# A hybrid encoder block with a gathered expert layer: how its place tiles are made, how many parked groups run per query tile, and how its weights and rows are buffered

## The chip, the cores and the metric

The kernel runs on one core of one Trainium2 chip. The metric is device microseconds (us) of one execution. TensorE is PE in the profile (PEld is its weight load), VectorE is DVE, ScalarE is ACT, GpSimd is POOL, SyncE is SP.

## The reference

One encoder layer on 1024 tokens of width 1024: adaLN, two token mixers (grouped attention and a bidirectional state-space scan) merged by gates, then a PEER expert layer, then a last norm. The part that matters here is PEER:

```python
q = (xt @ w_query).reshape(T, 8, 2, 128)
s1, s2 = scores of both halves of q against 128 keys each      # per head
v1, i1 = top_k(s1, 16); v2, i2 = top_k(s2, 16)
sc, pos = top_k(all sums v1 + v2, 16)                          # 16 of 16384 experts
idx = (i1 * 128 + i2)[pos];  g = softmax(sc)
a = gelu(einsum('thkd,td->thk', u_tab[idx], xt))
out = einsum('thk,thkd->td', g * a, v_tab[idx])
```

## The kernel before, in words

All products of weights and activations are made in three products of halves (`mm3`, L192): a float32 operand is split into a high part (ACT, a cast) and a low part (source less high part, on POOL or DVE), and PE adds high x high, high x low and low x high. `weights` (L178) loads one 128 x 1024 weight tile in two half loads through `wr` (three buffers) and splits it into whole tiles `wh` and `wl` (two buffers each).

PEER treats the tokens in two ways. The first TB = 384 tokens (three blocks of 128) are *fetched*: for each of 128 slots, POOL gathers one row of u for each token (128 x 1024, 512 KB) into a row buffer `br`, DVE makes the dot product with the token's activations (L1189), and after all slots rows of v are gathered four at a time and added by PE (`add`, L1220). The generator `fetched` (L1156) writes this order: a gather is written when the list `ahead` of unread rows holds no more than NROW - 1 = 8, with NROW = 9 buffers.

The other 640 tokens are *dense*: all 16384 experts, as 128 chunks of 128, are computed for all of them. `hidden_parts(c)` (L1303) makes gelu(u h) of a chunk in four parts, a quarter of its 48 matmuls of 320 columns each; the two halves of the tokens (j) one after the other, each with its own PSUM tile `hb`. Its weights are loaded two chunks ahead: `load` (L1293) at a chunk's end, and the low halves (`lows`) in the middle of the next. 88 chunks (PARKED, L72, spread evenly over the 128) are made early as filler and stored to `a_d` (L1325); the others are made when they are used.

The stages around the change: (1) query tiles, L1421: for each of 16 tiles m, two products of the query, the scores of the tile before, and four parts of a parked chunk. (2) the top 16 per score on DVE (`top`, L991) and the routing of blocks (`route`, L1034: DVE with products `ro` on POOL, L1085). (3) placing, L1482: the routed experts of four tokens become a one-hot pair of tiles `quad` (L1329): DVE compares a row of 0..127 (`iota`, which lies in PSUM) with both coordinates of all four tokens in one instruction over 1024 columns; then the second half is weighted by the gate (`weighted`, L1335), on POOL for two quads of four (one instruction over 512 columns), on ACT for the others (four of 128). PE multiplies the pair (`place`, L1342), ACT copies the result to `stg`, and 64 tokens at a time go to `G_d`. GB = 6 `quad` buffers. (4) the last stage, L1580 on: groups of EG = 3 chunks, each a live or parked chunk times its places, times v, added to `acc`; the fetching goes on beside it.

PE, DVE and POOL run in the order in which the program is written in stages 1 to 3 (`manual`, L1404), DVE and POOL in stage 4. That order comes from a planner with three clocks, at_pe, at_dve and at_dma: each written piece adds its assumed time (a part 1.73, a routing step ROUTE 2.5, a top TOP 1.8, a quad QUAD 1.7, a gather DGET 1.6). `hide` (L1386) writes parts of parked chunks while PE's clock is behind DVE's, until all but HOLD = 8 parts are written; `follow` (L1406) writes tops and routing steps while DVE's is behind PE's; `feed` (L1356) writes gathers while the transfers' clock is behind both, once the first block is routed, and adds 1.25 to DVE's clock for a u row and 0.46 to PE's for a v row.

Of the kernel before, what the change touches and what calls it, by code (L numbers as in the profile page):

```python
# [20 lines left out]
D = 1024  # L21
# [8 lines left out]
CUTS = [(0, TQ)] + [(TQ + j * W2, W2) for j in range(NJ)]  # L30
# [3 lines left out]
NPARK = 88  # L34
BSTEP = 3
FSTEP = 2
NROW = 9
# [4 lines left out]
QPOOL = 2  # L42
# [6 lines left out]
GB = 6  # L49
# [10 lines left out]
WH = 2  # L60
WL = 2
# [10 lines left out]
PARKED = [c for c in range(128) if (c + 1) * NPARK // 128 > c * NPARK // 128]  # L72
# [46 lines left out]
def block(ctx, tc, A, out, dbg=None):  # L119
# [58 lines left out]
    def weights(src, kd, eng=None, late=None):  # L178
        hi = wp.tile([128, 8, 128], FR, name="wh", bufs=WH)
        lo = wp.tile([128, 8, 128], FR, name="wl", bufs=WL)  # L180
        for k in range(0, kd, 4):
            raw = wp.tile([128, 4, 128], F32, name="wr", bufs=WR)
            nc.sync.dma_start(raw, src[:, k:k + 4])
            if late is None:
                split(raw, hi[:, k:k + 4], lo[:, k:k + 4], eng and eng[k // 4])
                continue
            ACT.copy(hi[:, k:k + 4], raw)  # L187
            late.append(lambda k=k, raw=raw: ((eng and eng[k // 4]) or POOL).tensor_tensor(  # L188
                lo[:, k:k + 4], raw, f32(hi[:, k:k + 4]), op=OP.subtract))
        return hi, lo  # L190
# [606 lines left out]
    bg = bp.tile([128, NB, 128], F32, name="bg")  # L797
    hx = pool("hx")
# [157 lines left out]
    kr = rt.tile([128, N_KR], F32, name="kr")  # L956
    nc.sync.dma_start(kr, A["kr"])
    for nm, x in zip("hl", (xh, xl)):
        for p, a in zip(x, others(nm, FR)):
            p[1] = a  # L960
    h2h, h2l = ([x[m][1] for m in range(8)] for x in (xh, xl))
    ip = pool("ip", "right")
    bw = pool("bw", "right")
    best = [bw.tile([128, 4, 2, 8, 16], F32, name="best", bufs=2) for _ in range(2)]
# [69 lines left out]
    def route(blk):  # L1034
# [66 lines left out]
        if blk < NB:  # L1101
            V.tensor_copy(bidx[:, blk], exf)
            V.tensor_copy(bx[:, blk], exf)
            V.tensor_copy(bg[:, blk], gf)
            ready.append(blk)
            yield
            return
# [19 lines left out]
    def final(p, src, t0, n, x1):  # L1127
        tl = slice(t0, t0 + n)
        nc.sync.dma_start(x1, x1_d[:, :, tl])
        yield "w"  # L1130
        yield "w"
        yield "w"
        for m in range(8):
            V.scalar_tensor_tensor(x1[:, m], src[:, m // 4, m % 4], mod[:, 40 + m:41 + m], x1[:, m], op0=OP.mult, op1=OP.add)
        yield "w"
        o = wide()
        acc = o[:, 0]
        for m in range(0, 8, 2):
            some = []
            for _ in range(2):  # L1140
                some.append(p.tile([128, n], F32, name="fsq", bufs=2))
# [12 lines left out]
        nc.sync.dma_start(out[:, :, tl], x1)  # L1154

    def fetched():  # L1156
# [5 lines left out]
        def rows(tab, idx):  # L1162
            r = rt.tile([128, D], F32, name="br", bufs=NROW)
# [8 lines left out]
        for b in range(NB):  # L1172
# [4 lines left out]
            yield from drain(NROW - 1)  # L1177
            st = rt.tile([128, D], F32, name="br", bufs=NROW)
            nc.sync.dma_start(st, h2t_d[b])
# [18 lines left out]
            def weights_of(b=b, a=a, aT=aT):  # L1198
                ACT.activation(a, a, AF.Gelu_apprx_tanh)
                yield "w"  # L1200
                V.tensor_tensor(a, a, bg[:, b], op=OP.mult)
# [4 lines left out]
                PE.transpose(o[:, :128], a, ident)  # L1206
                ACT.copy(aT, o[:, :128])

            ahead.append((1, begin))
            for s in range(128):  # L1210
                yield from drain(NROW - 1)
                r = rows("u", bidx[:, b, s:s + 1])
                ahead.append((1, lambda s=s, r=r, dot=dot: dot(s, r)))
                if s == 96:
                    flipped()
# [4 lines left out]
            def add(i, R, aT=aT, acc=acc):  # L1220
# [3 lines left out]
                if i % VG == 0:  # L1224
                    ACT.copy(z[:, :, 31:31 + 32 * VG:32], aT.rearrange("p (g i) -> p g i", g=4)[:, :, i:i + VG])
                at = 31 + 32 * (i % VG) - i
                for h in range(2):
                    for g in range(4):
                        PE.matmul(acc[0][32 * g:32 * g + 32, h], lhsT=z[:, g, at:at + 32], rhs=R[g][:, h * 512:(h + 1) * 512],  # L1229
                                  start=(i == 0), stop=(i == 31))  # L1230
# [3 lines left out]
            def finish(b=b, acc=acc):  # L1234
# [8 lines left out]
                x1 = rt.tile([128, 8, 128], F32, name="bacc")  # L1243
                yield from final(rt, o, b * 128, 128, x1)

            for i in range(32):
                R = []
                for g in range(4):
                    yield from drain(NROW - 1 - g)
                    R.append(rows("v", ixt[:, 32 * g + i:32 * g + i + 1]))  # L1250
# [26 lines left out]
    la.release()  # L1277
    dn = pool("dn")
# [3 lines left out]
    sources = [x for m in range(16) for x in (A["wq"][m], A["uT"][order[m]])] + [A["uT"][c] for c in order[16:]]  # L1282
# [10 lines left out]
    def load():  # L1293
        lows()
        src = next(sources, None)
        if src is not None:
            loaded.append(weights(src, 8, halves_by, late))

    load()
# [3 lines left out]
    def hidden_parts(c):  # L1303
        uh, ul = loaded.popleft()
        a = dn.tile([128, TA], F32, name="a", bufs=2)
        done = 0
        for j in range(NJ):
            o = psE.tile([128, 512], F32, name="hb", bufs=2)[:, :W2]
            js = slice(j * W2, (j + 1) * W2)
            for kd in range(8):  # L1310
                mm3(o, (uh[:, kd], ul[:, kd]), (h2h[kd][:, js], h2l[kd][:, js]), kd == 0, kd == 7)
                done += 1
                if done == 4 * NJ:
                    lows()
# [20 lines left out]
    def weighted(x, ig, t):  # L1335
        if t // 4 % 4 < QPOOL:
            POOL.tensor_tensor(x[:, 1], x[:, 1], ig[:, 2, t:t + 4].unsqueeze(2).to_broadcast([128, 4, 128]), op=OP.mult)
        else:
            for j in range(4):
                ACT.activation(x[:, 1, j], x[:, 1, j], AF.Identity, scale=ig[:, 2, t + j:t + j + 1])  # L1340
# [80 lines left out]
    for m in range(17):  # L1421
# [15 lines left out]
        if m < 16:  # L1437
            for _ in range(4):
# [42 lines left out]
    compared = []  # L1481
    for t in range(TB, S, 4):  # L1482
        blk = t // 128
        made.append((t - TB, quad(crossed[blk], t % 128)))
        if compared:
            weighted(*compared.pop())
        compared.append((made[-1][1], crossed[blk], t % 128))
# [7 lines left out]
    weighted(*compared.pop())  # L1495
# [133 lines left out]
    for m in range(8):  # L1629
        x1 = rt.tile([128, TA], F32, name="br", bufs=NROW)  # L1630
# [4 lines left out]
    def last(m, j, js, o):  # L1635
        x = acc[:, m, js]
        V.scalar_tensor_tensor(x, o, mod[:, 40 + m:41 + m], x, op0=OP.mult, op1=OP.add)
        sq = rt.tile([128, W2], F32, name="br", bufs=NROW)
# [14 lines left out]
    dn.release()  # L1653
    hx.release()
# [64 lines left out]
```

## Time and profile before

| what | value |
|---|---|
| runs shown, median (lowest, highest) | 4068.97 us (4056.01, 4076.5), three runs |
| the profiled execution, its time | 4056.31 us |
| its span | 4054.5 us |
| mean granted clock of PE | 0.953 |
| busy, share of the span | PE 90%, DVE 64%, POOL 45%, ACT 33% |
| 16 transfer engines | 211 GB/s over the span, 854 MB |

A busy time is the time in which an engine had at least one instruction running. A wait is the idle time of an engine in front of an instruction, put down to what ended last before it. In the tables of windows the count of instructions stands in brackets, and the granted clock is a share of full speed.

### The profile page before, as it was taken

The numbers are of one execution on the slowest core, as the hardware profiler recorded it, in microseconds if no ns is written. First come the engines' busy times: TensorE is split into PE (matmuls) and PEld (weight loads), VectorE is DVE, ScalarE is ACT, GpSimd is POOL, SyncE is SP. The second block draws the span as 40 slices with busy tenths as digits, with TensorE's granted clock in tenths as the row PEclk, the third lists the DMA queues.
The fourth block names the chain that finished last, engine by engine and source line by source line (L and its number), as shares of the span: only waits on it lengthen the run. The fifth ranks groups of instructions, "written<-read, shape, count | busy, mean of one in ns | idle before, by whom it ended". The sixth has DMA issues, their size and how long they took to land.

```text
span 4054.5 us, 61036 instructions
## 1 busy us (share of the span) xinstructions
PE 3660.2 (90%) x22927; PEld 3204.8 (79%) x22927; DVE 2578.8 (64%) x5316; ACT 1339.1 (33%) x2659; POOL 1812.5 (45%) x1529
## 2 busy tenths in 40 slices
PE   5799999998899899679888888999999899999998
PEld 4577777776688799678677788999788899978887
DVE  5698951347672678934785556489444698864456
ACT  4265542223323432122225655422222222222222
POOL 3211112565454567736776545444444343434420
PEclk8899999998899999789998999999999999999999
DMA  5111124323375349944776777888898798889962
GB/s 182 37 46 46 50 89 142 109 92 121 116 231 175 104 165 318 346 164 148 252 250 209 269 270 273 313 284 297 315 315 309 251 314 284 298 293 318 312 231 87
DMA packets 387784, 854.04 MB, mean 211 GB/s; under 512 B 32800, under 2 KB 146976, under 8 KB 384672
## 3 DMA queue, kind: packets, MB, share of 16 engines
q1 hardware_dynamic: 276896, 447.44, 32.5%
q0 software_dynamic: 110592, 402.70, 28.6%
q8 instruction: 180, 2.95, 0.3%
q14 instruction: 116, 0.95, 0.1%
HBM read 740.44 MB, written 109.58 MB: 210 GB/s over the span
## 4 chain that ended last, share of the span: by engine, by line
PE 33%; DVE 9%; DMA 8%; issue 2%; ACT 2%; POOL 2%; SPq 0%; ACTq 0%; POOLq 0%; DVEq 0%
PE pb L195 4%; PE pb L194 4%; PE pb L196 4%; PE hb L194 4%; DMA vr<-v 4%; PE hb L196 4%; PE gx L1229 4%; PE hb L195 4%; PE pb L1346 3%; DVE br L1189 3%; DMA G_d<-stg 2%; PE io L194 1%; PE io L195 1%; DVE Wl L1545 1%; PE io L196 1%
## 5 line engine op out<-in xcount | busy, mean ns | idle before, releaser
L196 PE MATMUL hb<-ah,wl 128*128 128x320 f32 x2048 | 649.3, 317 | 59.5 <-POOL wl L188 41.1
L194 PE MATMUL hb<-ah,wh 128*128 128x320 f32 x2048 | 661.1, 323 | 19.3 <-ACT a L1317 19.1
L195 PE MATMUL hb<-al,wh 128*128 128x320 f32 x2048 | 646.4, 316 | 0.0
L1164 POOL DMA_INDIRECT br<-u,bidx x384 | 366.5, 955 | 470.0 <-DVE br L1189 330.1
L1164 POOL DMA_INDIRECT br<-v,ixt x384 | 381.1, 992 | 425.9 <-PE gx L1229 303.4
L174 POOL TENSOR_TENSOR wl<-wr,wh 128x512 fp32r<-128x512 f32 x170 | 230.0, 1367 | 673.1 <-ACT wh L173 617.7
L194 PE MATMUL pb<-Wh,vh 128*128 128x320 f32 x1536 | 473.6, 315 | 16.3 <-ACT Wh L1542 11.8
L195 PE MATMUL pb<-Wl,vh 128*128 128x320 f32 x1536 | 479.0, 313 | 9.5 <-DVE Wl L1545 9.4
L196 PE MATMUL pb<-Wh,vl 128*128 128x320 f32 x1536 | 476.3, 311 | 0.0
L1189 DVE SCALAR_TENSOR_TENSOR br<-br,gx 128x1024 f32<-128x1024 f32 x384 | 454.9, 1215 | 30.3 <-DMA br<-u,bidx 27.7
L196 PEld LDWEIGHTS hb<-ah,wl 128*128 128x128 f32 x2048 | 396.8, 194 | 67.3 <-POOL wl L188 45.1
L194 PEld LDWEIGHTS hb<-ah,wh 128*128 128x128 f32 x2048 | 398.2, 194 | 48.9 <-issue 24.0
L188 POOL TENSOR_TENSOR wl<-wr,wh 128x512 fp32r<-128x512 f32 x269 | 343.2, 1296 | 201.2 <-ACT wh L187 198.7
L195 PEld LDWEIGHTS hb<-al,wh 128*128 128x128 f32 x2048 | 397.8, 194 | 0.0
L1575 DVE TENSOR_TENSOR acc<-acc,pb 128x320 f32<-128x320 f32 x492 | 229.8, 485 | 209.1 <-PE pb L196 207.8
L187 ACT CAST wh<-wr 128x512 fp32r<-128x512 f32 x288 | 177.1, 618 | 560.4 <-DMA wr<-uT 303.9
L173 ACT CAST vh<-vr 128x512 fp32r<-128x512 f32 x256 | 150.9, 618 | 614.1 <-PE pb L195 395.1
L194 PEld LDWEIGHTS pb<-Wh,vh 128*128 128x128 f32 x1536 | 288.1, 190 | 43.5 <-ACT Wh L1542 16.7
L195 PEld LDWEIGHTS pb<-Wl,vh 128*128 128x128 f32 x1536 | 290.7, 189 | 17.7 <-DVE Wl L1545 14.2
L1331 DVE TENSOR_TENSOR quad<-io,rig 128x1024 f32<-128x1024 f32 x160 | 190.4, 1221 | 166.6 <-PE pb L1346 105.1
L196 PEld LDWEIGHTS pb<-Wh,vl 128*128 128x128 f32 x1536 | 290.4, 189 | 0.2
L194 PE MATMUL w<-hh,wh 128*128 128x512 f32 x560 | 230.1, 411 | 8.2 <-ACT zg L548 4.3
(362 smaller groups left out, 8235.6 us busy)
## 6 DMA issues: line engine op xcount, KB each, us to landing
wr<-uT SPq DMA_DIRECT2D x256, 256.0 KB, 4.5
vr<-v SPq DMA_DIRECT2D x256, 256.0 KB, 5.7
G_d<-stg SPq DMA_DIRECT2D x20, 2048.0 KB, 12.2
gt<-G_d SPq DMA_DIRECT2D x42, 960.0 KB, 6.5
a_d<-a SPq DMA_DIRECT2D x88, 320.0 KB, 4.4
a<-a_d SPq DMA_DIRECT2D x88, 320.0 KB, 5.9
wr<-wi SPq DMA_DIRECT2D x82, 256.0 KB, 2.7
sq<-adaT SPq DMA_DIRECT2D x32, 512.0 KB, 4.3
```

What stands on the lines that cost most here:

```text
L173: ACT.copy(hi, src)
L174: (eng or POOL).tensor_tensor(lo, src, f32(hi), op=OP.subtract)
L187: ACT.copy(hi[:, k:k + 4], raw)
L188: late.append(lambda k=k, raw=raw: ((eng and eng[k // 4]) or POOL).tensor_tensor(lo[:, k:k + 4], raw, f32(hi[:, k:k + 4]), op=OP.subtract))
L194: PE.matmul(o, lhsT=wh, rhs=xh, start=first, stop=False)
L195: PE.matmul(o, lhsT=wh, rhs=xl, start=False, stop=False)
L196: PE.matmul(o, lhsT=wl, rhs=xh, start=False, stop=last)
L1164: POOL.indirect_dma_start(out=r, out_offset=None, in_=A[tab], in_offset=bass.IndirectOffsetOnAxis(ap=idx, axis=0))
L1189: V.scalar_tensor_tensor(v2(r), v2(r), 1.0, hrow[0], op0=OP.mult, op1=OP.mult, accum_out=a[:, s:s + 1])
L1229: PE.matmul(acc[0][32 * g:32 * g + 32, h], lhsT=z[:, g, at:at + 32], rhs=R[g][:, h * 512:(h + 1) * 512], start=(i == 0), stop=(i == 31))
L1331: V.tensor_tensor(x, iota.unsqueeze(1).unsqueeze(1).to_broadcast([128, 2, 4, 128]), ig[:, 0:2, t:t + 4].unsqueeze(3).to_broadcast([128, 2, ...
L1575: V.tensor_tensor(acc[:, m, js], acc[:, m, js], o, op=OP.add)
```

## The change

With TB = 384 the new constant TH is 0, so all code under `if TH`, and the branches for a half block in `fetched` and `final`, are never taken; CUTS keeps its values. What is left:

- `quad` makes the first half with one compare over 512 columns and the second with one compare-and-multiply of 128 columns per token, all on DVE; `weighted` is gone; GB is 5.
- PARKED is every chunk but the first of each group of three: 85 instead of 88. Eight parts are written per query tile, not four, and `sources` has two chunks after each query tile.
- `wh` and `wl` are half tiles with four buffers each. `hidden_parts` runs the first half of the weights for both j, then the second half for both; a half is reloaded when both j have used it.
- NROW is 10, and the list `ahead` may hold NROW - 1 - SLACK = 7. The row buffers lie in a pool `rg` of their own.

```diff
-NROW = 9
+NROW = 10
+SLACK = 2
-GB = 6
+GB = 5
-WH = 2
-WL = 2
+WH = 4
+WL = 4
-PARKED = [c for c in range(128) if (c + 1) * NPARK // 128 > c * NPARK // 128]
+PARKED = [c for c in range(128) if c % EG]
+NPARK = len(PARKED)
...
+    def weight_half(src, k, hi, lo, eng=None, late=None):
+        raw = wp.tile([128, 4, 128], F32, name="wr", bufs=WR)
+        nc.sync.dma_start(raw, src[:, k:k + 4])
+        h = wp.tile([128, 4, 128], FR, name="wh", bufs=WH)
+        w = wp.tile([128, 4, 128], FR, name="wl", bufs=WL)
...
+        ACT.copy(h, raw)
+        late.append(lambda: (eng or POOL).tensor_tensor(w, raw, f32(h), op=OP.subtract))
...
-                yield from drain(NROW - 1)
-                r = rows("u", bidx[:, b, s:s + 1])
+                yield from drain(NROW - 1 - SLACK)
+                r = rows("u", at_idx[:, s:s + 1])
...
-    sources = [x for m in range(16) for x in (A["wq"][m], A["uT"][order[m]])] + [A["uT"][c] for c in order[16:]]
+    sources = [x for m in range(16) for x in (A["wq"][m], A["uT"][order[2 * m]], A["uT"][order[2 * m + 1]])]
+    sources += [A["uT"][c] for c in order[32:]]
...
-        for j in range(NJ):
-            o = psE.tile([128, 512], F32, name="hb", bufs=2)[:, :W2]
+        turn[0] = NJ - 1 - turn[0]
+        first = [abs(turn[0] - j) for j in range(NJ)]
+        o = {}
+        parts = [(j, k) for k, js in ((0, first), (1, first[::-1])) for j in js]
+        for n, (j, k) in enumerate(parts):
+            if not k:
+                o[j] = psE.tile([128, 512], F32, name="hb", bufs=2)[:, :W2]
             js = slice(j * W2, (j + 1) * W2)
-            for kd in range(8):
-                mm3(o, (uh[:, kd], ul[:, kd]), (h2h[kd][:, js], h2l[kd][:, js]), kd == 0, kd == 7)
-                done += 1
-                if done == 4 * NJ:
-                    lows()
-                if done % (2 * NJ) == 0 and done < 8 * NJ:
-                    yield None
-            ACT.activation(a[:, js], o, AF.Gelu_apprx_tanh)
-        load()
-        yield a
+            for kd in range(4 * k, 4 * k + 4):
+                mm3(o[j], (uh[:, kd], ul[:, kd]), (h2h[kd][:, js], h2l[kd][:, js]), kd == 0, kd == 7)
+            if k:
+                ACT.activation(a[:, js], o[j], AF.Gelu_apprx_tanh)
+            if n in (0, 2):
+                lows()
+            if n in (1, 3):
+                load(n // 2)
+            yield a if n == 3 else None
...
-        V.tensor_tensor(x, iota.unsqueeze(1).unsqueeze(1).to_broadcast([128, 2, 4, 128]),
-                        ig[:, 0:2, t:t + 4].unsqueeze(3).to_broadcast([128, 2, 4, 128]), op=OP.is_equal)
+        V.tensor_tensor(x[:, 0], iota.unsqueeze(1).to_broadcast([128, 4, 128]),
+                        ig[:, 0, t:t + 4].unsqueeze(2).to_broadcast([128, 4, 128]), op=OP.is_equal)
+        for j in range(4):
+            V.tensor_scalar(x[:, 1, j], iota, ig[:, 1, t + j:t + j + 1], ig[:, 2, t + j:t + j + 1], op0=OP.is_equal, op1=OP.mult)
...
-            for _ in range(4):
+            for _ in range(8):
                 parked_part()
                 follow(0.0)
```

## Rows read from the trace of the kernel before

**Rows 1.** Windows by stage: busy time of each engine (instructions), PEclk, DMA share, GB/s.

```profile
1500.00:1600.00 100.00, 98.57 (x689) 98.30 (x688) 89.76 (x315) 29.16 (x66) 75.45 (x71) 1.00 0.90 314
1600.00:1650.00 50.00, 34.29 (x222) 34.02 (x221) 45.74 (x132) 9.65 (x21) 33.78 (x35) 0.83 0.89 332
1700.00:1750.00 50.00, 28.56 (x163) 28.03 (x162) 45.76 (x173) 6.30 (x12) 32.34 (x33) 0.73 0.88 343
1905.00:2146.00 241.00, 207.86 (x1341) 166.69 (x1341) 177.05 (x565) 58.50 (x113) 191.95 (x149) 0.94 0.74 243
2146.00:2570.00 424.00, 372.01 (x2753) 347.77 (x2754) 250.86 (x280) 246.92 (x754) 232.69 (x221) 0.92 0.72 260
2660.00:2850.00 190.00, 178.13 (x1182) 174.65 (x1181) 167.41 (x299) 45.32 (x79) 75.89 (x75) 0.99 0.87 292
2850.00:3200.00 350.00, 347.43 (x2395) 289.51 (x2394) 172.98 (x296) 75.85 (x139) 151.58 (x148) 1.00 0.89 309
```

**Rows 2.** Waits of PE, 1320 to 1905 us: total, times, longest.

```profile
PE pb L196 <- POOL wl L188: 32.9, 3, 15.7
PE hb L196 <- POOL wl L188: 22.9, 3, 14.0
```

**Rows 3.** Instructions of POOL in order of time, 1608 to 1638 us: start, length.

```profile
1608.23 0.95 POOL L1164 DMA_INDIRECT br<-u,bidx  x1
...
1633.08 0.94 POOL L1164 DMA_INDIRECT br<-u,bidx  x1 [0.31 <-DVE best L995]
1634.04 3.74 POOL L188 TENSOR_TENSOR wl<-wr,wh 128x512 fp32r<-128x512 f32 x3
```

**Rows 4.** Waits of DVE, 1700 to 1905 us.

```profile
DVE re L1078 <- POOL ro L1085: 107.6, 4, 102.6
```

**Rows 5.** Stores of parked chunks on SP's queue, in order of time: start, length.

```profile
1443.81 0.42 SPq L1325 DMA_DIRECT2D a_d<-a  x1
...
1466.59 0.33 SPq L1325 DMA_DIRECT2D a_d<-a  x1
...
1481.79 0.33 SPq L1325 DMA_DIRECT2D a_d<-a  x1
...
1758.31 0.40 SPq L1325 DMA_DIRECT2D a_d<-a  x1
...
1864.03 0.33 SPq L1325 DMA_DIRECT2D a_d<-a  x1
```

**Rows 6.** Waits of PE, 1905 to 2146 us.

```profile
PE hb L196 <- DVE wl L188: 17.2, 7, 5.5
PE hb L196 <- POOL wl L188: 9.6, 9, 1.9
```

**Rows 7.** Groups of instructions, whole span: busy us, mean ns, idle before and what ended it.

```profile
L1189 DVE SCALAR_TENSOR_TENSOR br<-br,gx 128x1024 f32<-128x1024 f32 x384 | 454.9, 1215 | 30.3 <-DMA br<-u,bidx 27.7 <-ACT gx L1184 2.2
...
L1331 DVE TENSOR_TENSOR quad<-io,rig 128x1024 f32<-128x1024 f32 x160 | 190.4, 1221 | 166.6 <-PE pb L1346 105.1 <-issue 26.2 <-ACT quad L1340 11.1
...
L1317 ACT ACTIVATE a<-hb 128x320 f32<-128x320 f32 x256 | 109.3, 434 | 184.0 <-PE hb L196 77.3 <-issue 54.8 <-DVE Wl L1545 39.9
...
L1340 ACT ACTIVATE quad<-quad,rig 128x128 f32<-128x128 f32 x320 | 103.5, 398 | 23.1 <-DVE quad L1331 22.7
...
L1189 DVE DVE_READ_ACCUMULATOR br<-br,gx 128x1 f32 x384 | 32.2, 84 | 0.0
```

**Rows 8.** Waits of PE, 2146 to 2570 us.

```profile
PE pb L1346 <- ACT stg L1349: 28.7, 8, 5.3
...
PE pb L1346 <- POOL quad L1337: 8.4, 1, 8.4
```

**Rows 9.** Line 207, VectorE reading PSUM: ns min/median/max, first and last start, shapes.

```profile
L207 DVE TENSOR_SCALAR rstd<-pb x8: 248/420/426, 26.6 to 1322.9; 128x256 f32<-128x256 f32 x6, 128x96 f32<-128x96 f32 x1, 128x160 f32<-128x160 f32 x1
L207 DVE TENSOR_SCALAR rstd<-gx x3: 181/184/185, 2410.3 to 3935.4; 128x32 f32<-128x32 f32 x3
```

**Rows 10.** Instructions of VectorE in order of time, from 2401 us.

```profile
2401.37 2.16 DVE L1134 SCALAR_TENSOR_TENSOR bacc<-gx,mod,bacc 128x128 f32<-128x128 f32 x8 [2.01 <-DMA bacc<-x_d]
```

More of the change, by code (lines that the diff above doesn't have):

```diff
@@ L41 @@
 TOP = 1.8
-QPOOL = 2
 RSTEPS = 18
@@ L797, in block @@
     bg = bp.tile([128, NB, 128], F32, name="bg")
+    if TH:
+        hidx = bp.tile([128, 64], I32, name="hidx")
+        hg = bp.tile([128, 64], F32, name="hg")
     hx = pool("hx")
@@ L960, in block @@
             p[1] = a
+            if TH:
+                (ACT.copy if nm == "h" else POOL.tensor_copy)(a[:, :TQ - TB], f32(p[0])[:, TB:])
     h2h, h2l = ([x[m][1] for m in range(8)] for x in (xh, xl))
@@ L963, in block @@
     bw = pool("bw", "right")
+    kr = bw.tile([128, N_KR], F32, name="kr")
+    nc.sync.dma_start(kr, A["kr"])
     best = [bw.tile([128, 4, 2, 8, 16], F32, name="best", bufs=2) for _ in range(2)]
@@ L1140, in final @@
             for _ in range(2):
-                some.append(p.tile([128, n], F32, name="fsq", bufs=2))
+                some.append(p.tile([128, 128], F32, name="fsq", bufs=2)[:, :n])
                 ACT.activation(some[-1], x1[:, m + len(some) - 1], AF.Square)
@@ L1176, in fetched @@
             aT = rt.tile([128, 128], F32, name="aT")
-            yield from drain(NROW - 1)
-            st = rt.tile([128, D], F32, name="br", bufs=NROW)
-            nc.sync.dma_start(st, h2t_d[b])
+            yield from drain(NROW - 1 - SLACK)
+            st = rg.tile([128, D], F32, name="br", bufs=NROW)
+            half = 128 * b + 128 > TB
+            if half:
+                for k in range(2):
+                    nc.sync.dma_start(st[64 * k:64 * k + 64], h2t_d[b, 0:64])
+            else:
+                nc.sync.dma_start(st, h2t_d[b])
+            at_idx, at_g = (hidx, hg) if half else (bidx[:, b], bg[:, b])
+            slots = 64 if half else 128
             hrow = []
@@ L1242, in finish @@
                     PE.transpose(o[:, m // 4, m % 4], s[:, m * 128:(m + 1) * 128], ident)
-                x1 = rt.tile([128, 8, 128], F32, name="bacc")
-                yield from final(rt, o, b * 128, 128, x1)
-            for i in range(32):
+                x1 = rt.tile([128, 1024], F32, name="bacc")[:, :8 * n].rearrange("p (m t) -> p m t", m=8)
+                yield from final(rt, o, b * 128, n, x1)
+            for i in range(steps):
                 R = []
                 for g in range(4):
-                    yield from drain(NROW - 1 - g)
-                    R.append(rows("v", ixt[:, 32 * g + i:32 * g + i + 1]))
+                    yield from drain(NROW - 1 - SLACK - g)
+                    R.append(rows("v", ixt[:, steps * g + i:steps * g + i + 1]))
                     yield "v"
@@ L1291, in lows, with load @@
             late.pop(0)()
-    def load():
-        lows()
-        src = next(sources, None)
-        if src is not None:
-            loaded.append(weights(src, 8, halves_by, late))
+    def load(half=None):
+        if half != 1:
+            src = next(sources, None)
+            if src is not None:
+                loaded.append((Halves(), Halves()))
+                coming.append(src)
+        for k in (0, 1) if half is None else (half,):
+            lows()
+            if coming:
+                weight_half(coming[0], 4 * k, *loaded[-1], halves_by and halves_by[k], late)
+                if k:
+                    coming.pop()
+    coming = []
     load()
@@ L1653, in block @@
     dn.release()
+    rg.release()
     hx.release()
```

93 lines of the change are left out of this document (49 added, 44 removed).

## The prediction

> **What bounds the kernel now.** I read the windows by stage first [rows 1]. From 1500 to 1600 us TensorE (PE) is 98.6% busy; then it falls to 34.3 of 50 us and 28.6 of 50 us at a granted clock of 0.83 and 0.73, and VectorE (DVE) is busy for over 90% of these two windows. In routing (1905 to 2146) and placing (2146 to 2570) no engine is full: placing has PE at 372.0, DVE at 250.9 and ScalarE (ACT) at 246.9 of 424 us. In the last stage PE is full again: idle 11.9 us of 190 where u rows are fetched and 2.6 us of 350 where v rows are. So what can be won lies between 1600 and 2570 us.
>
> The waits of PE say why it starves there: 32.9 us in three waits of a query tile and 22.9 us in three waits of a chunk for `wl`, the low half of a split weight, made by POOL [rows 2]. The POOL list shows what `wl` stands behind: a run of 21 u gathers from 1608.23 to 1633.08, one per 1.24 us, then three splits at once [rows 3]. DVE has the opposite hole a little later, 107.6 us in four waits for POOL's `ro` product [rows 4]: there the list of POOL holds the splits of some sixteen chunks that PE runs back to back, one per 7.05 us [rows 5]. The two holes are one fault of order: too little PE work was written into the query tiles, so the planner first writes gathers in a bunch and then chunks in a bunch.
>
> I walked the planner's sums through the code (part 1.73, ROUTE 2.5, TOP 1.8, DGET 1.6). Before, 53 u gathers are issued by the end of the 12th tile and 115 by the 16th, 15 a tile at the end; 64 parts are written in the tile loop and 65 more during the 15 scores left over. After, the gathers stand at 19, 56, 93 and 129 after 4, 8, 12 and 16 tiles, 9 a tile, and 128 of the 133 parts that are written by then stand inside the loop.
>
> **The change part by part.** The sum is made against the profiled execution, 4056.3 us (span 4054.5); the median of the runs, 4069.0, is 12.7 us above it.
>
> *Two chunks per query tile.* Before, the store of the first parked chunk starts at 1443.81 and that of the 32nd at 1864.03: 420.2 us [rows 5]. A tile with one chunk takes 15.20 us (1466.59 to 1481.79) and a chunk alone 7.05 (15 steps from 1758.31 to 1864.03), so a tile with two takes 22.25 us if PE stays full. The 32nd store is then 7.05 + 15 x 22.25 = 340.8 us behind the first: 79 us won. The other bound is transfers: a tile moves three weight tiles (1.57 MB), two stores (0.66) and 9.1 gathers of 0.52 MB (4.79), 7.02 MB; at the 292 GB/s of 2660 to 2850 [rows 1] that is 24.0 us a tile, and 53 us won; at the 314 and 343 GB/s of 1500 to 1750 it is 22.4 and 20.5, no more than PE's time. POOL has 9.1 x 1.24 + 6 x 1.25 = 18.8 us of work per tile plus its share of `ro`, so it has little slack either. I take 23.6 us, near the slow end: 361 us, **59 won**. DVE does the same list in it, without the 107.6 us hole. The four half loads and the store that each added chunk issues move past nothing but other weight loads on SP's queue; they are in the 7.02 MB.
>
> *Half weight tiles, and the order of the four parts.* A chunk's first half is now reloaded after its second part, and its split is due five parts before its use, not two. In the query stage this is part of the 59. In routing the waits for `wl` are 17.2 and 9.6 us [rows 6]: between 0 and 27 won. I take 0, because PE, 33 us idle there, is not what sets the pace: the planner writes some 15 parts for each routed block, before and after, and DVE and POOL hand the `ro` products to and fro; a wait less on PE then becomes a longer wait for the next place in the order. The added cost: both PSUM halves of a chunk are open to its end, so the next chunk may wait for a gelu of 0.43 us [rows 7]; with 16 back-to-back pairs in the tiles that is 0 to 7 us, covered by the gap between 22.25 and 23.6.
>
> *Placing.* Removed are 320 ACT instructions, 103.5 us [rows 7], and 80 of POOL. What PE waits for there is 28.7 us of ACT's `stg` copies, which stay, and 8.4 us of a weighting on POOL, once, at the stage's start [rows 8]; both engines have idle time left, so the removal itself is put at 0 (8 at most). DVE's compare of 1024 columns, 1221 ns, becomes one of 512 and four of 128. The one of 512: 1221 less 512 columns at 1.05 ns (the slope below) is 0.68 us, in a row less. For a two-operand TENSOR_SCALAR of 128 columns with its input in PSUM there is no row; its neighbours are 184 ns for 32 columns and 420 ns for 256 [rows 9], a slope of 1.05 ns and 285 ns at 128. Neighbouring instructions overlap: eight of 128 columns and 343 ns each fill 2.16 us, 0.27 each [rows 10], which scales 285 to 225. Bounds per four tokens: 0.62 + 4 x 0.184 = 1.36 and 0.68 + 4 x 0.285 = 1.82 us, against 190.4 / 160 = 1.19 now [rows 7]: +27 to +101 us of DVE. I take 0.68 + 0.90 = 1.58, **+62 us**, between the two because the overlap is shown.
>
> [...]
>
> The walk also moves 38 u gathers forward: 85 of the second block's are issued by the end of placing, not 47. Each dot is 1.22 + 0.08 us [rows 7]: +49 us of DVE. DVE's work in placing is then 251 + 62 + 49 = 362 us. Its idle time there is 173 us, 105.1 of it for a quad buffer that PE has not emptied [rows 7]. That wait goes when quads come slower than PE takes them (five buffers instead of six are then enough); the other 68 stay. 362 + 68 = 430 against 424: **+6 us**. Bounds: 392 (30 us idle) and 535 (173 idle).
>
> *Last stage.* The 38 dots were spread at 190 us per some 64 of them, 113 us of the stage with 6% of PE idle instead of 1%: -6. Only 8 parts (before 21) are left to hide the first read of the places: 0 to 15 us, I take 4. Together **-2**.
>
> *Ten row buffers, two slack.* A gather is issued when 7 rows wait (before 8) and reuses a buffer whose reader was written three steps earlier, not one. POOL blocks less, with one row less in flight; on the critical path 0, because the blocked time is POOL's and PE waits for POOL only through `wl`, counted above. 85 parked chunks instead of 88, and every group of three with just one live chunk: 0 within a few us.
>
> Sum: -59 + 0 + 6 - 2 = -55: 4001 us for the profiled execution, 4014 from the median. I forecast **4008**.
>
> **The rivals.** *Place stage bound by DVE (slower).* If DVE's order, not the buffers, makes its idle time, all 173 us stay and placing takes 535 us: +111 - 61 = +50, 4106 us. It decides when DVE is idle for more than 485 - 362 = 123 us in placing. For it: 362 us of work would be the most of any engine there but PE. Against: 105 of the 173 name PE. 13%. [...]
>
> *Cover used up (no change).* The limit of 332 written parts is reached in the last 32 quads: in the walk PE's clock ends at 893 and DVE's at 942. If PE truly stands for these 49 us and nothing later is shorter for it, -59 + 55 - 2 = -6: 4050 us, with slack prefetch that does nothing included. For it: total PE work is the same, so each idle us counts. Against: the gathers written there are owed by the last stage. 18%.
>
> *Larger gain.* PE full in the tiles (-79), `wl` waits gone in routing (-27), placing at 392 (-32), the last stage -6: -144; halfway from the forecast to that is -100: 3956 us. 16%.
>
> **How the numbers follow.** Forecast 53% (its own range 3975 to 4040). A measurement of this kernel can tell some 0.5% (20 us) from no change. Faster: 53 + 16 less 1 for its upper edge = 68%; same 18 + 1 = 19%; slower 13%. The range from 3945 to 4070 leaves out the slower rival's upper part (12%) and gains beyond 110 us (8%).
>
> **What would show it.** Stores of the 1st and 32nd parked chunk some 361 us apart, clock 1.0 and PE over 93% busy through the query tiles, no DVE hole for `ro`, few waits of PE for `wl`: the first step right. DVE per quad 1.58 us, DVE idle in placing near 70 us, the place stage 420 to 440 us: the third. The forecast is wrong if the tiles take over 25 us, or if placing grows by more than 40 us.

## The result, and the profile after

The changed kernel takes 4012.2 us (median of four runs, 4009.5 to 4014.5) against 4065.1 us of before (four runs, 4056.0 to 4076.5): a ratio of 0.986 (95% interval 0.984 to 0.989), 53 us faster. Forecast were 4008 us, 61 less than the median of 4069 shown with the kernel of before. The profiled execution after took 4010.0 us (span 4008.3, mean granted clock 0.958).

The stages are cut at four marks that both traces have: the stores of the 1st and of the 32nd parked chunk, the first `quad`, and the last copy of `stg`. One correction is due here: counted through, the store at 1864.03 in [rows 5] is the 33rd; the 32nd starts at 1857.0. The prediction's 420.2 us for the query tiles were therefore 413.2.

| stage (us) | before | after | change | forecast |
|---|---|---|---|---|
| 1st to 32nd store (query tiles) | 413.2 | 345.9 | -67.3 | -59 |
| to the first `quad` (routing) | 289.6 | 299.5 | +9.9 | 0 |
| placing | 415.2 | 436.9 | +21.7 | +6 |
| last stage | 1492.7 | 1480.3 | -12.4 | -2 |
| sum | | | -48.1 | -55 |

(What lies ahead of the first store is 1.9 us longer, so the span is 46.2 shorter.) Stages are read from one profiled execution of a kernel each. That of before is the fastest of its four, 9 us below their median, so a difference of some 10 us in placing or the last stage can be chance; the query tiles repeat within 1 us (344.9 to 345.9 in the eight kernels below and above that share them).

The windows by stage of the kernel after, with the columns of [rows 1]:

```profile
1500.00:1600.00 100.00, 100.00 (x696) 100.00 (x695) 81.20 (x305) 30.82 (x64) 75.58 (x71) 1.00 0.92 326
1600.00:1650.00 50.00, 50.00 (x348) 49.95 (x347) 44.84 (x158) 17.72 (x34) 35.83 (x34) 1.00 0.88 313
1700.00:1750.00 50.00, 50.00 (x348) 49.99 (x347) 39.82 (x132) 15.00 (x32) 39.30 (x37) 1.00 0.90 319
1850.00:2091.00 241.00, 213.76 (x1375) 165.21 (x1367) 188.21 (x566) 59.45 (x111) 194.06 (x151) 0.97 0.76 247
2091.00:2528.00 437.00, 375.98 (x2778) 355.70 (x2776) 394.25 (x978) 162.57 (x439) 171.61 (x166) 0.93 0.76 281
2528.00:2708.00 180.00, 148.96 (x944) 144.41 (x944) 128.65 (x219) 48.05 (x91) 70.96 (x66) 0.91 0.88 300
```

The two windows where PE starved, 34.3 and 28.6 us of 50 at a granted clock of 0.83 and 0.73 [rows 1], are full: 50.00 of 50 at clock 1.00. What was won there is partly given back below: in placing DVE is now busy for 394 of 437 us (before 251 of 424), and at the start of the last stage PE is idle for 31 us of 180.

The stores of parked chunks on SP's queue after (start, length) show the new pitch, to be held against [rows 5]:

```profile
1445.73 0.33 SPq L1381 DMA_DIRECT2D a_d<-a  x1
...
1516.56 0.33 SPq L1381 DMA_DIRECT2D a_d<-a  x1
...
1538.80 0.33 SPq L1381 DMA_DIRECT2D a_d<-a  x1
...
1791.60 0.33 SPq L1381 DMA_DIRECT2D a_d<-a  x1
```

A tile with two chunks takes 22.24 us (1516.56 to 1538.80), which is 15.20 + 7.04: PE's own time and nothing else. The mean of all fifteen tiles is 22.59 us, and PE is busy for 343.7 of the 345.9 us.

The waits of PE after (total, times, longest), 1320 to 1810 us, in place of [rows 2], where `wl` stood with 32.9 and 22.9 us:

```profile
PE pb L1002 <- ACT q L992: 14.1, 15, 1.0
PE hb L204 <- ACT a L1368: 5.2, 3, 3.0
```

No wait for `wl` is left. The one for the gelu was there before, with 11.2 us in two waits from 1320 to 1905 us, and is 9.1 us over that stretch now. The wait of DVE for POOL's `ro`, 107.6 us in [rows 4], is now 18.7 us over the longer stretch of 1320 to 1905 us. In its place DVE waits longer for the scores, which come from PE through ACT (87.7 us, before 42.3 in the same stretch):

```profile
DVE best L1010 <- ACT s L1003: 87.7, 27, 11.4
DVE re L1093 <- POOL ro L1100: 18.7, 10, 3.3
```

Waits of PE after, 1850 to 2091 us (routing, [rows 6]):

```profile
PE hb L204 <- ACT a L1368: 15.4, 6, 5.9
PE gx L1270 <- DMA br<-v,ixt: 8.6, 7, 2.7
```

and 2091 to 2528 us (placing, [rows 8]):

```profile
PE pb L1397 <- DVE quad L1390: 16.5, 9, 3.3
PE pb L1397 <- ACT stg L1400: 13.8, 6, 3.9
PE hb L206 <- POOL wl L194: 12.9, 1, 12.9
PE gx L211 <- DVE bacc L1161: 11.9, 1, 11.9
```

In routing the `wl` waits (26.8 us) have gone too, but waits for the gelu and for rows of v stand in their place. In placing PE now waits for DVE's `quad` and, once, for DVE's `bacc`, 28 us together.

The groups of DVE after, whole span, in the columns of [rows 7]:

```profile
L1223 DVE SCALAR_TENSOR_TENSOR br<-br,gx 128x1024 f32<-128x1024 f32 x384 | 456.4, 1225 | 8.7 <-ACT gx L1218 6.2 <-DMA br<-u,bidx 2.4
...
L1390 DVE TENSOR_SCALAR quad<-io,rig 128x128 f32<-128x128 f32 x640 | 228.9, 475 | 0.0
...
L1387 DVE TENSOR_TENSOR quad<-io,rig 128x512 f32<-128x512 f32 x160 | 120.7, 754 | 26.1 <-PE pb L1397 26.1
```

and DVE's instructions in order of time (start, length; x4 joins four in a row):

```profile
2094.85 0.70 DVE L1387 TENSOR_TENSOR quad<-io,rig 128x512 f32<-128x512 f32 x1
2095.45 1.38 DVE L1390 TENSOR_SCALAR quad<-io,rig 128x128 f32<-128x128 f32 x4
2096.72 0.70 DVE L1387 TENSOR_TENSOR quad<-io,rig 128x512 f32<-128x512 f32 x1
2097.32 1.39 DVE L1390 TENSOR_SCALAR quad<-io,rig 128x128 f32<-128x128 f32 x4
2098.59 0.71 DVE L1387 TENSOR_TENSOR quad<-io,rig 128x512 f32<-128x512 f32 x1
```

Back to back, four tokens take 1.87 us (2094.85 to 2096.72): 0.60 for the compare of 512 columns and 4 x 0.318 for the tokens. The price is read from starts, not from the mean of 475 ns: records of neighbours overlap.

### The profile page after: what moved, and what is told of

Its sections match the earlier page's. It is cut to its first block, busy times and chain, and to the rows that moved or that the text cites. A ratio compares the mean times of both kernels' runs of the same rounds, so it can differ in the third digit from the quotient of the medians.

```text
span 4008.3 us, 61236 instructions
## 1 busy us (share of the span) xinstructions
PE 3641.6 (91%) x22927; PEld 3189.3 (80%) x22927; DVE 2716.1 (68%) x5956; ACT 1266.6 (32%) x2338; POOL 1739.7 (43%) x1449
## 4 chain that ended last, share of the span: by engine, by line
PE 32%; DVE 7%; DMA 6%; issue 4%; POOL 2%; ACT 1%; SPq 0%; ACTq 0%; DVEq 0%; POOLq 0%
PE pb L204 4%; DMA vr<-v 4%; PE pb L205 4%; PE pb L206 4%; PE gx L1270 4%; PE hb L204 3%; PE hb L205 3%; PE hb L206 3%; PE pb L1397 3%; DVE br L1223 2%; PE io L204 1%; PE io L205 1%; PE io L206 1%; DMA G_d<-stg 1%; POOL br L1191 1%
## 5 line engine op out<-in xcount | busy, mean ns | idle before, releaser
L204 PE MATMUL hb<-ah,wh 128*128 128x320 f32 x2048 | 652.4, 319 | 23.4 <-ACT a L1368 23.0
L206 PE MATMUL hb<-ah,wl 128*128 128x320 f32 x2048 | 640.1, 313 | 15.6 <-POOL wl L194 15.3
L194 POOL TENSOR_TENSOR wl<-wr,wh 128x512 fp32r<-128x512 f32 x269 | 352.4, 1315 | 531.6 <-ACT wh L193 501.6
L175 POOL TENSOR_TENSOR wl<-wr,wh 128x512 fp32r<-128x512 f32 x170 | 231.4, 1364 | 637.8 <-ACT wh L174 477.4
L175 DVE TENSOR_TENSOR vl<-vr,vh 128x512 fp32r<-128x512 f32 x256 | 201.8, 788 | 75.6 <-ACT vh L174 64.5
```

What stands on the lines that cost most here:

```text
L175: (eng or POOL).tensor_tensor(lo, src, f32(hi), op=OP.subtract)
L194: late.append(lambda: (eng or POOL).tensor_tensor(w, raw, f32(h), op=OP.subtract))
L204: PE.matmul(o, lhsT=wh, rhs=xh, start=first, stop=False)
L206: PE.matmul(o, lhsT=wl, rhs=xh, start=False, stop=last)
```

## The experiments

Ratios are to runs of before on the same chip, taken together with them, and a hundredth is 41 us. Kernels that ran on different chips are compared by their ratios; by the medians such a difference comes out up to 6 us otherwise. Experiments on "the changed kernel" have all of the change but for the edit.

### Two chunks per query tile: taken out, and alone

In the changed kernel, four parts and one chunk per tile again:

```diff
-    sources = [x for m in range(16) for x in (A["wq"][m], A["uT"][order[2 * m]], A["uT"][order[2 * m + 1]])]
-    sources += [A["uT"][c] for c in order[32:]]
+    sources = [x for m in range(16) for x in (A["wq"][m], A["uT"][order[m]])] + [A["uT"][c] for c in order[16:]]
...
-            for _ in range(8):
+            for _ in range(4):
```

> The changed kernel with one parked chunk per query tile again (four parts, one chunk in the load order); half weight tiles, ten row buffers and the new place tiles stay. Theory (the gain is the PE work moved into the tiles): the 32nd store again lies some 410 to 420 us behind the first, the hole of VectorE for the ro products returns with about 100 us, and the time is 4045 to 4070 us. Rival (the half weight tiles and the slack in the row buffers had already taken away the waits for wl): the waits of TensorE for wl stay near zero, the tiles end without loss, and the time is 4010 to 4025 us.

Measured: 4048.1 us, ratio 0.9943 (0.9923 to 0.9964). Its 1st and 32nd stores start at 1440.54 and 1860.72, 420.2 us apart, and the hole of DVE is back, as the theory says (waits of DVE from 1320 to 1905 us):

```profile
DVE re L1093 <- POOL ro L1100: 103.6, 6, 96.3
```

PE starves again beside it (window, columns as above):

```profile
1700.00:1750.00 50.00, 28.17 (x140) 25.52 (x138) 43.77 (x139) 6.18 (x14) 34.31 (x35) 0.69 0.93 349
```

The reverse edit alone, in the kernel of before:

> The kernel before with nothing changed but eight parts and two chunks per query tile. Theory: tiles of 22.3 to 22.8 us, the 32nd store some 345 us behind the first, and as placing keeps its old cost, 3995 to 4015 us, no slower than the full change. Rival (whole weight tiles can't be split in time at this rate): tiles of 24 us or more with waits of TensorE for wl of 40 us, 4030 to 4050 us.

Measured: 4008.0 us, ratio 0.9855 (0.9831 to 0.988): tiles 354.2 us, placing 429.5, last stage 1474.2. This one edit has the whole gain of the change. The rest of it (half tiles, order of parts, ten rows, new places and 85 parked chunks) is worth some 23 us without this edit, by the run above, and nothing beside it, so the two don't add up; the runs below take the rest apart, but for the half tiles, which were not tried by themselves.

### The places: old ones in the changed kernel, new ones alone, and a row of numbers in SBUF

The changed kernel with the compare of 1024 columns and `weighted` of before (GB stays 5):

> The changed kernel with the old place tiles (one compare over 1024 columns, weighting on GpSimd and ScalarE), still five quad buffers. Theory (the new place tiles cost time): VectorE's work in placing falls by 150 us, the place stage from 437 to 410 to 420 us, the time to 3985 to 4000 us. Rival (VectorE hides them and ScalarE and GpSimd are the better for it): the waits for the weighting return and the time is 4012 to 4035 us.

Measured: 4011.3 us, 0.9859 (0.9837 to 0.9881), against 0.9863 with the new places. The theory fails: DVE's work in placing falls by 109 us, as it should (285 for 394), but the stage does not get shorter. It takes 449.6 us against 436.9 (its profiled execution is the slowest of five, 6 us above the median), and the last stage 1472.7.

The new `quad` alone in the kernel of before:

> The kernel before with nothing changed but the place tiles (still six quad buffers). Theory: +160 us of VectorE in placing of which 85 are hidden where VectorE now stands idle for a buffer; 4075 to 4100 us. Rival (the removed work of ScalarE and GpSimd pays for it): 4045 to 4065 us.

Measured: 4067.9 us, 1.0004 (0.9989 to 1.002). The place stage is 404.6 us there, against 415.2 before, although DVE is busy for 353 us of it instead of 243; the last stage is 21 us longer, of two profiled executions that differ by 17 us where the medians differ by 1. So twice the new places change nothing in the time that can be measured, and twice the place stage is 11 to 13 us shorter with them: DVE's 109 us fit into its idle time. Whether the work that ACT and POOL are spared makes the stage shorter was not tried.

The third edit lets each token's compare read a copy of `iota` in SBUF:

```diff
+    iota_s = gp.tile([128, 128], F32, name="iota_s")
+    V.tensor_copy(iota_s, iota)
...
-            V.tensor_scalar(x[:, 1, j], iota, ig[:, 1, t + j:t + j + 1], ig[:, 2, t + j:t + j + 1], op0=OP.is_equal, op1=OP.mult)
+            V.tensor_scalar(x[:, 1, j], iota_s, ig[:, 1, t + j:t + j + 1], ig[:, 2, t + j:t + j + 1], op0=OP.is_equal, op1=OP.mult)
```

> The changed kernel with a copy of the row 0..127 in SBUF as the input of the compare-and-multiply per token (the compare over 512 columns still reads PSUM). Theory (an input from PSUM makes the instruction slow): 120 to 230 ns a token instead of 318, VectorE's work in placing falls by 55 to 125 us and the time to 3985 to 4003 us. Rival (the two scalars per partition make it slow): still 300 ns or more, 4008 to 4016 us; a second rival is that VectorE then waits for GpSimd's instructions, with single instructions of over 1 us.

Measured: 4001.8 us, 0.9852 (0.9832 to 0.9872). DVE's instructions in order of time in this kernel:

```profile
2096.72 0.68 DVE L1387 TENSOR_TENSOR quad<-io,rig 128x512 f32<-128x512 f32 x1
2097.32 1.10 DVE L1390 TENSOR_SCALAR quad<-iota_s,rig 128x128 f32<-128x128 f32 x4
2098.34 0.68 DVE L1387 TENSOR_TENSOR quad<-io,rig 128x512 f32<-128x512 f32 x1
```

Four tokens take 1.62 us and one token (1.62 - 0.60) / 4 = 0.256 us instead of 0.318, which would free 40 us of DVE in placing. The trace shows only 11: DVE is busy there for 383 us instead of 394. The second rival is why. Of the 640 records 22 last over 1 us (none with the input in PSUM), and each of the 22 ends 0.08 to 0.09 us after a split of `wl` on POOL. The row of all 640, with their shortest, median and longest in ns:

```profile
L1390 DVE TENSOR_SCALAR quad<-iota_s,rig x640: 325/335/2439, 2092.4 to 2524.8; 128x128 f32<-128x128 f32 x160
```

The longest, 2.44 us from 2313.97, lies beside two splits in a row (2313.80 to 2316.31). The mean distance of two tokens is therefore 0.305 us, not 0.256: over 640 tokens this takes back 31 of the 40 us. By the ratios the time falls by 4 us, by the medians by 10, and the interval overlaps that of the changed kernel.

### The order of the parts, and the tenth row

The changed kernel with the old order in `hidden_parts` (all of one half of the tokens, then the other, both halves of the weights loaded at the chunk's end), half tiles kept:

> The changed kernel with the old order of a chunk's four parts (one half of the tokens after the other, weights reloaded at the chunk's end); half weight tiles stay as tiles. Theory: TensorE's waits for wl come back with 15 to 40 us, most of them in routing, and the time is 4012 to 4030 us. Rival (the new order only makes each chunk wait for the gelu of the one before): the waits for the gelu fall from some 22 us to under 5, 3995 to 4010 us.

Measured: 4032.4 us, 0.9922 (0.9906 to 0.9938): the new order is worth 24 us. But not where the prediction looked for it: up to the first `quad` this kernel is even 7 us earlier (2083.6 against 2091.1). It loses 18 us in placing (455.4) and 10 in the last stage (1490.7). In routing PE waits for `wl` again, 11.5 us in seven waits, and less for the gelu, 8.5 us against 16.9 (1800 to 2100 us): one wait in place of the other. The theory has the time within 3 us of its range, and not the place.

The changed kernel with nine rows and no slack:

```diff
-NROW = 10
-SLACK = 2
+NROW = 9
+SLACK = 0
```

> The changed kernel with nine row buffers and no slack, as before. Theory (GpSimd's blocked time is off the path once the gathers are spread): 4005 to 4020 us, with 100 us more of GpSimd's waits for the dots. Rival (a gather that waits for its buffer holds up the wl behind it): waits of TensorE for wl of 20 us or more and 4025 to 4045 us.

Measured: 4025.2 us, 0.9903 (0.9887 to 0.992): row and slack are worth 16 us, 15 of them in placing (452.2 us). It lies above the theory's range and at the lower end of the rival's, but the rival's waits of PE for `wl` are 22.1 us in all from 1440 us on, against 15.3 with ten rows: 7 us more, and with nine rows all of them lie behind placing. POOL's waits in front of a gather, 1440 to 2545 us, first in the changed kernel:

```profile
POOL br L1191 <- ACT gx L1218: 30.2, 1, 30.2
POOL br L1191 <- DVE br L1223: 15.6, 19, 2.9
POOL br L1191 <- PE gx L1270: 10.8, 3, 8.3
```

and with nine rows:

```profile
POOL br L1191 <- PE gx L1270: 72.5, 10, 17.9
POOL br L1191 <- DVE br L1223: 70.7, 44, 11.5
...
POOL br L1191 <- ACT gx L1218: 23.6, 1, 23.6
```

With nine rows POOL stands blocked for 167 us by rows that DVE, PE or ACT have not read, with ten for 57. Both kernels also show ACT's `stg` copies waiting longer for the store of the buffer before them; the waits of ACT for it from 2084 to 2545 us, in the changed kernel, then with the old order, then with nine rows:

```profile
ACT stg L1400 <- DMA G_d<-stg: 13.9, 8, 2.9
```

```profile
ACT stg L1397 <- DMA G_d<-stg: 25.8, 9, 5.1
```

```profile
ACT stg L1400 <- DMA G_d<-stg: 24.2, 9, 8.9
```

PE's waits for those copies in placing are 13.8, 24.8 and 22.6 us. So both edits show at the stores of the places. What makes these late, and whether this is the whole of the 16 and 24 us, was not tried.

### Parts kept back for the last stage

In the changed kernel 24 parts instead of 8 are kept back for the start of the last stage:

```diff
-HOLD = 8
+HOLD = 24
```

> The changed kernel with 24 parts kept back from the end of placing, not 8. Theory (TensorE needs them at the start of the last stage more than at the end of placing): the 92 us after placing lose 5 us of TensorE idle time instead of 26, placing grows by less than 10 us, and the time is 3995 to 4008 us. Rival (the parts are only moved from one bare place to the next): 4008 to 4016 us.

Measured: 4044.9 us, 0.9958 (0.9943 to 0.9972): 33 us slower than the changed kernel (39 by the ratios). Placing is 476.0 us, 39 more, and the last stage 1480.3, as before the edit. By the time, the theory that the start of the last stage wants parts is out. But the edit moves two things. Where the planner may write no part, the transfers' clock is not moved on and it writes gathers: with 16 parts fewer in placing there are 30 dots more. DVE's dots in placing, in the changed kernel and then with 24 parts kept back:

```profile
L1223 DVE SCALAR_TENSOR_TENSOR br<-br,gx 128x1024 f32<-128x1024 f32 x77 | 93.6, 1265 | 5.0 <-ACT gx L1218 5.0
```

```profile
L1223 DVE SCALAR_TENSOR_TENSOR br<-br,gx 128x1024 f32<-128x1024 f32 x107 | 125.3, 1210 | 3.5 <-ACT gx L1218 3.5
```

DVE's work in placing is 35 us more (429 of 476 us) and its idle time 47 us against 43, so DVE's work accounts for most of the 39 us; PE's waits for `quad` grow with it, from 16.5 us to this:

```profile
PE pb L1397 <- DVE quad L1390: 60.8, 24, 3.3
```

Likewise the last stage got 16 parts more and 30 dots less, so that its length stays says nothing of either alone. The end of placing in the changed kernel (windows, columns as above):

```profile
2500.00:2531.00 31.00, 14.75 (x83) 13.29 (x82) 31.00 (x66) 6.28 (x20) 17.91 (x19) 0.64 0.95 358
2531.00:2562.00 31.00, 12.06 (x68) 11.80 (x66) 7.29 (x13) 7.75 (x13) 10.98 (x10) 0.67 0.92 332
```

PE is busy for less than half of these 62 us, and its granted clock, 0.64 and 0.67 in the mean, reads 0.50 for 43 of them. DVE is busy for all of the first 31.

### The number of parked chunks

The changed kernel with the old list of 88 (then with 94 in the same formula, then with 88 and the copy of `iota` in SBUF):

```diff
-PARKED = [c for c in range(128) if c % EG]
-NPARK = len(PARKED)
+NPARK = 88
+PARKED = [c for c in range(128) if (c + 1) * NPARK // 128 > c * NPARK // 128]
```

> The changed kernel with the old list of 88 parked chunks in place of 85, all else kept. Theory (cover): what the change costs behind the query tiles comes from the three chunks that are no longer parked, 12 parts that PE lacks at the end of placing and at the start of the last stage (there PE is busy for 149 of 180 us from 2528 to 2708, against 165 in the kernel that only has two chunks per tile and 88 parked). Placing plus the 180 us behind it should give back 12 parts of 1.76 us or more, 20 us: 3985 to 3998, query tiles unchanged at 346. Rival (total work): a part costs PE the same wherever it stands, so the place stage gets shorter and the last stage longer by the same, 4005 to 4015, not told from the changed kernel.

Measured: 3984.9 us, 0.9802 (0.9789 to 0.9816): 25 us faster than the changed kernel by the ratios, and query tiles as they were (345.3 us). Placing is 423.4 us (-13.5), the last stage 1462.2 (-18.1; the profiled execution is the fastest of five, 11 us below their median). The end of placing in this kernel:

```profile
2300.00:2528.00 228.00, 212.13 (x1549) 210.51 (x1550) 188.05 (x449) 84.49 (x222) 102.69 (x94) 0.96 0.80 294
2500.00:2531.00 31.00, 29.48 (x207) 29.02 (x205) 2.89 (x6) 8.86 (x21) 12.51 (x12) 1.00 0.86 324
```

and the first of these windows in the changed kernel:

```profile
2300.00:2528.00 228.00, 193.77 (x1367) 188.88 (x1365) 214.52 (x494) 77.22 (x208) 110.92 (x107) 0.91 0.83 308
```

Two things happen at once. PE has parts to the end, at clock 1.00; and since the planner counts a part's transfers, it writes fewer gathers beside them: DVE makes 59 dots in placing instead of 77, and its work there falls from 394 to 374 us, on the engine that is nearly full. The run does not part the two.

> The changed kernel with 94 parked chunks in place of 85, spread as evenly. Theory (cover): the planner's deficit at the end of placing is 49 us, some 28 parts or 7 chunks, so the gain over 85 goes on to about 92 and then stops: some 10 us below the run with 88, 3975 to 3990. Rival (transfers): each parked chunk adds a store and a load of 0.33 MB each, and takes live work from the last stage, whose DMA is busy for over 80% of the time: with nine more chunks, 5.9 MB or 20 us at 290 GB/s, the last stage grows and the kernel stands at 4010 to 4030.

Measured: 4011.7 us, 0.9858 (0.984 to 0.9876): the six chunks more lose it all again. Neither expectation is met to the end. Placing does not change, 423.6 us, and nor do its dots, 62 for 59, so six chunks more give nothing there: 29 stores of parked chunks start in placing, and 8 behind it, against 30 and 1 with 88 chunks (28 and none with 85). What cannot be used there is made at the start of the last stage, with a store and a load that a live chunk does not have (858.0 MB in all, 854.1 with 88), and in 9 groups instead of 3 no live chunk is left for PE to do beside the loads. The last stage is 1499.8 us, 38 longer than with 88 in the two profiled executions, whose medians differ by 27. Which of the two, transfers or groups without a live chunk, was not separated.

> The changed kernel with 88 parked chunks and the compare of each token reading an SBUF copy of the row of numbers. If the two effects are separate, it takes 5 to 15 us off the run with 88 parked alone (the copy took 10 us off the changed kernel, 386 against 476 ns a record); if DVE no longer sets the pace once cover is there, it is the same as 88 alone within 5 us.

Measured: 3976.6 us, 0.9775 (0.976 to 0.9791), the fastest version here, 2.2% below before and 0.9% below the changed kernel. Against 88 alone it is 8 us less; the two intervals just touch.

Last, 85 chunks in the kernel that has two chunks per tile and nothing else of the change:

> The kernel of before with two chunks per query tile (4008 as measured alone) and 85 parked chunks instead of 88, nothing else of the change. Theory (cover): the three chunks are cover whatever else stands, so the 27 us that they gave the changed kernel are lost here too: 4025 to 4040, placing and the first 180 us of the last stage 20 us longer together. Rival: 85 costs only beside the ten rows and the dearer places of the changed kernel, whose VectorE is busy for 90% of placing; here VectorE is idle for 168 us of 429 in placing and takes the time up: 4003 to 4013.

Measured: 4026.2 us, 0.9933 (0.9917 to 0.9948), with before at 4050.2 on that chip, so ratios are compared: 0.9855 with 88, 0.9933 with 85, 32 us. Placing is 14 us longer and the last stage 12. The rival, that DVE's idle time takes it up, falls: here DVE is busy for only 277 of 437 us (2091 to 2528), and yet the stage grows, with 78 dots in it against 58. The two windows ahead of and behind the end of placing, in the kernel with two chunks per tile and 88 parked:

```profile
2300.00:2528.00 228.00, 204.57 (x1535) 202.53 (x1536) 153.87 (x204) 126.97 (x376) 136.86 (x130) 0.94 0.76 272
2528.00:2708.00 180.00, 165.21 (x1064) 161.01 (x1063) 129.50 (x217) 51.03 (x97) 66.71 (x65) 0.96 0.87 300
```

and with 85:

```profile
2300.00:2528.00 228.00, 193.14 (x1377) 191.13 (x1376) 162.46 (x224) 116.18 (x343) 137.88 (x134) 0.92 0.80 293
2528.00:2708.00 180.00, 148.92 (x934) 144.16 (x935) 131.69 (x217) 50.27 (x101) 71.68 (x69) 0.90 0.86 300
```

PE loses 11 and 16 us of busy time in them.

The kept traces show what goes with the length of placing, first for kernels with the new places, then with the old (parts are PE's matmuls of `hb` in the stage by 12):

| kernel | dots in placing | parts | DVE busy, us | placing, us |
|---|---|---|---|---|
| new places alone | 40 | 97 | 353 | 404.6 |
| one chunk per tile | 42 | 100 | 355 | 405.0 |
| 88 chunks | 59 | 114 | 374 | 423.4 |
| 94 chunks | 62 | 113 | 377 | 423.6 |
| changed kernel | 77 | 107 | 394 | 436.9 |
| 24 parts kept back | 107 | 91 | 429 | 476.0 |
| 88 chunks, row of numbers in SBUF | 57 | 109 | 360 | 411.8 |
| 85 chunks, row of numbers in SBUF | 77 | 107 | 383 | 435.0 |
| before | 41 | 95 | 243 | 415.2 |
| two chunks per tile alone | 58 | 110 | 261 | 429.5 |
| the same, 85 chunks | 78 | 105 | 283 | 443.7 |
| changed, old places | 79 | 108 | 285 | 449.6 |

The number of parts does not order the lengths; the number of dots does, at about 1 us each, in both halves of the table. Nine rows and the old order have the changed kernel's dots and parts and are 15 and 18 us above this. So the kernel that runs out of parts pays, as far as the traces tell, through the dots that are written in their place. No run changed the dots alone.

## Why the prediction was right, and where it was not

**Query tiles: right, and too cautious.** The mechanism is shown from both sides: two chunks per tile alone gives 0.9855, the change without them 0.9943. Of the bounds for a tile, 22.25 us (PE full) and 24.0 us (transfers at 292 GB/s), the first held: 22.24 us for most tiles, PE 100% busy from 1500 to 1650 and 1700 to 1750 us, 313 to 326 GB/s. The 23.6 that I took was a compromise for which no row spoke; the rows of 1500 to 1750 us with 314 and 343 GB/s did speak, and were from the same stretch. Forecast 59 won, measured 67.3. The miscount of one store made the 420.2 us seven too long and hid a part of it: after, the forecast was 361 us and the tiles take 345.9.

**Routing: 0 forecast, 9.9 lost.** As argued, the waits for `wl` went and others took their place. The gelu wait was priced for the query tiles alone, at 0 to 7 us, and is 5.2 there; in routing, where nothing was put down for it, it is 15.4. The loss belongs to the two chunks per tile: this stage takes 298.8 us where they are the only edit, 289.1 where they alone are taken out, and 296.7 with the old order of parts. What of it is one wait and what another was not taken apart.

**Placing: +6 forecast, +21.7 measured; two terms were wrong.** The price per four tokens was 1.58 us with bounds of 1.36 and 1.82; it is 1.87, above both, +109 us of DVE instead of +62. The step that failed in it is the discount: 285 ns, from the 184 and 420 ns of another TENSOR_SCALAR [rows 9], scaled down to 225 by an instruction whose input is the same but whose operation is not [rows 10]. This form takes 318 ns from PSUM, 33 more than the neighbours gave even without the discount, and 256 from SBUF. On the time the dearer form had no effect, since the old places cost as much (0.9859 to 0.9863). Nor did this term lengthen the stage, which is 11 to 13 us shorter with the new places in both pairs of runs. The other term is the dots: 36 more (77 for 41; 38 forecast) came as the walk said, but they were to be paid for by the wait for PE's buffer together with the new places. The traces show about 1 us of stage for each, as two chunks per tile alone (17 dots more, 14 us) and 85 chunks there (20 more, 14 us) do. DVE's work is 394 us (362 forecast), its idle time 43 (68 forecast): the sum of 437 against 430 is near by luck, because the two errors cancel. The wait for PE's buffer was forecast to go and fell from 105.1 us to 26.1.

**85 chunks instead of 88: "0 within a few us" was the failed step.** It costs 25 us in the changed kernel and 32 in the one with two chunks per tile. The prediction had the means to see it: its rival *cover used up* says that parts run out in the last 32 quads and that PE then stands for 49 us. Twelve parts fewer had to be priced there, at a part's 1.76 us or more, 21 us at least. That rival describes a part of what happens, PE standing at the end of placing; that the planner then writes dots in place of the parts, 18 to 20 more for 85 chunks than for 88, it left out, and the loss comes from three chunks that the change itself took away.

**Ten rows and the order of parts: 0 each forecast, 16 and 24 won.** Both gain in placing, where the prediction looked only for what PE waits for on POOL. These two and the 85 chunks nearly cancel, which is luck: the sum came out within 5 us of the median for reasons of which some are wrong.

**The rivals.** *Place stage bound by DVE* did not come as written: DVE is idle for 43 us, far from the 123 at which it decides, although its work was more than forecast. Still the stage follows DVE's dots, by the table above. *Larger gain* is out by the time, but its first part (PE full in the tiles) is what happened, and with 88 chunks and the SBUF copy 89 us are won.

**Last stage: -2 forecast, -12.4 measured.** The dots moved ahead are 36 where 38 were forecast. The prediction has no term for the parts that are made in this stage: the trace has 180 there where before had 191, 19 us of PE at 1.76 us each. That these make the other 10 us was not tried, and the profiled executions alone can differ by as much.

## What to carry to other kernels

Filler that hides another engine's work has a price where it runs out, not where it is made (here 25 us for three chunks, with query tiles of 345.9 and 345.3 us): count what is left of it at the end of the last stage that needs it, and what the planner writes there instead, before calling three chunks more or fewer nothing. When a price is needed for an instruction form that no row shows, don't discount for overlap that another operation showed, and don't take the span of its neighbours for a bound: here 318 ns stood above the 285 that they gave. And a change whose parts cancel looks like a change with one effect: one run with the main part alone shows whether there is more to be had, here 36 us.

## What the runs showed that was not expected

The same instruction form leaves records of different length in different executions while its starts stay where they are: the compare of a token has a median of 460 ns in the changed kernel and 401 ns in the one with 88 chunks, yet four tokens take 1.87 us in both. With its input in SBUF the record's median is 335 ns, and some reach 2439, beside POOL's splits, which none with the input in PSUM does (641 at most). So 40 us less by the price of four tokens were 11 us less of DVE's work.
